# Output projections: a normed tile's transposes half a tile of products later, the last two tiles' inside the MLP's first unit, four normed-row buffers

## The chip, the cores and the metric

The kernel runs on one core of one Trainium2 chip. The metric is the device time of one execution in microseconds. Three timed runs of the kernel before gave 1408.19, 1409.34 and 1409.35 us, median 1409.34.

## What is computed (the reference, cut)

A two-layer encoder for one sequence of 512 positions with 1024 columns in float32. Layer 0 mixes tokens by dilated sliding-window attention, layer 1 by latent attention. Each mixer ends in an output projection that is added to the residual, and after it come a norm and a squared-ReLU MLP. The change lies at this seam, which occurs twice:

```python
def rms_norm(x, gain):
    xf = x.astype(jnp.float32)
    y = xf * lax.rsqrt(jnp.mean(xf * xf, axis=-1, keepdims=True) + EPS)
    return (y * gain.astype(jnp.float32)).astype(x.dtype)

def sq_relu_mlp(h, w1, w2):
    a = jax.nn.relu(h @ w1)
    return (a * a) @ w2

    for i in range(DEPTH):
        h = rms_norm(x, norm_mix[i])
        ...
            y = dilated_mixer(...)   # layer 0; ends in  o @ w_o
            y = mla_mixer(...)       # layer 1; ends in  o @ w_o
        x = x + y
        h = rms_norm(x, norm_ffn[i])
        x = x + sq_relu_mlp(h, ffn_w1[i], ffn_w2[i])
```

## The kernel before

**Numbers.** Every float32 operand of a product is split in two: `hi`, a rounded copy written by ACT, and `lo`, the rest, written by DVE as operand minus `hi`. Each product is made of three: hi·hi, hi·lo, lo·hi. Weights are loaded by SP as `raw` units of 256 rows by 512 columns (three buffers), split by `load_unit` (L158 on ACT, L159 on DVE) into `whi` and `wlo` (four buffers each).

**The projection (`project`, L920).** The 512 positions are four row tiles of 128. The output's 1024 columns are made in two blocks of 512. The second block holds all its weights, four units, and goes tile by tile: 8 slices of the inner dimension times 3 products, 24 products a tile (L183, from `block_groups`), into one of four `acc` banks. When a tile is done, DVE adds it to the residual (`resid`, L926), and `norm_tile` (L210) norms the row tile: ACT squares and sums (L138), DVE adds epsilon (L130), POOL raises to -1/2 (L133), DVE writes the normed row `xn` (L216). `norm_tile` returns a function `turn` that transposes the row: eight transposes on PE (L125) into two `tp` banks, of which there are only two, and out of each bank ACT copies `hi` (L226) and DVE subtracts `lo` (L227) into `hT_f`, the MLP's operand. The text calls the eight transposes of a row tile its turn.

**What sets the order.** A scheduler puts each engine's instructions in order by its own simulation. `tc.issue_after(ins)` binds the instructions issued inside it behind `ins` on the same engine. Before the change, tile 2's products were bound behind turn 0, tile 3's behind turn 1, and the MLP's first unit behind turn 2. Turn 3 was left to the scheduler.

**The MLP (`mlp`, L876).** Its first unit `up(0, 0)` takes its four weight units at once and works in two halves: first all products with columns 0 to 255 of `hT_f` (row tiles 0 and 1), 96 products of 256 columns, then those with columns 256 to 511 (row tiles 2 and 3). The later units follow one after another, with the second weight matrix loaded into `wqs` (on the memory of the projection's operand) and used by `down`.

Of the kernel before, what the change touches and what calls it, by code (L numbers as in the profile page):

```python
# [20 lines left out]
NT = S // P  # L21
# [67 lines left out]
def encoder_kernel(ctx: ExitStack, tc: tile.TileContext, x, norm_mix, norm_ffn, a_w_qkv, a_q_gain, a_k_gain,  # L89
# [3 lines left out]
    V, A, G, PE = nc.vector, nc.scalar, nc.gpsimd, nc.tensor  # L93
    uid = [0]
    marks = {}

    def nm(s):
        uid[0] += 1
        return f"{s}_{uid[0]}"
# [27 lines left out]
    def rstd_of(ss, n, add, name, out=None):  # L127

        v = st.tile([P, 8], F32, tag="rs_v", name=nm("rs_v"))
        V.tensor_scalar(v[:, :n], ss, add, None, op0=ALU.add)  # L130
        if out is None:
            out = st.tile([P, 8], F32, tag=name, name=nm(name))[:, :n]
        G.tensor_tensor(out, v[:, :n], nhalf[:, :n], op=ALU.pow)  # L133
        return out

    def mean_square(junk, x, dim, out):

        A.activation(junk, x, AF.Square, scale=1.0 / math.sqrt(dim), accum_out=out)  # L138
# [12 lines left out]
    def load_unit(src, nk, dims, n, home=None, raw=None):  # L151

        if raw is None:
            raw = load_raw(src, nk, dims, n)
        if home is None:
            home = [wp.tile([P, 2, 512], F32R, tag=t, name=nm(t)) for t in ("whi", "wlo")]
        hi, lo = home
        A.activation(hi[:, :nk, :n], raw[:, :nk, :n], AF.Copy)  # L158
        V.tensor_tensor(lo[:, :nk, :n], raw[:, :nk, :n], hi[:, :nk, :n].bitcast(F32), op=ALU.subtract)  # L159
        return hi, lo, nk  # L160

    def block_groups(units, groups, n, mm, outs=NT, halves=1, raws=None, order=None):

        accs = [acc_p.tile([P, 512], F32, tag="acc", name=nm("acc")) for _ in range(outs)]
        total = sum(u[1] for u in units)
        ui = 0
        kt0 = 0
        for gi, g in enumerate(groups):
            loaded = []
            for _ in range(g):  # L170
                src, nk, dims = units[ui]
                loaded.append(load_unit(src, nk, dims, n, raw=raws[ui] if raws else None))
                ui += 1
            first = [kt0 + sum(x[2] for x in loaded[:i]) for i in range(g)]
            kt0 = first[-1] + loaded[-1][2]
            steps = order or [(hv, o, u) for hv in range(halves) for o in range(outs) for u in range(g)]
            left = {o: g * halves for o in range(outs)}
            for hv, o, u in steps:
                hi, lo, nk = loaded[u]
                for j in range(nk):  # L180
                    kt = first[u] + j
                    for p_i, (lt, rt, oc) in enumerate(mm(o, kt, hi[:, j], lo[:, j], hv)):
                        PE.matmul(accs[o][:, oc], lhsT=lt, rhs=rt, start=(kt == 0 and p_i == 0 and hv == 0),  # L183
                                  stop=(kt == total - 1 and p_i == 2), skip_group_check=halves > 1)
                left[o] -= 1
                if gi == len(groups) - 1 and not left[o]:
                    yield o, accs[o]
            if gi < len(groups) - 1:
                yield None

    def run_block(units, groups, n, mm, evac, outs=NT, halves=1, order=None):
        for end in block_groups(units, groups, n, mm, outs, halves, order=order):
            if end is not None:
                evac(*end)

    def act_stationary(hT, n, own={}):

        def mm(r, kt, hi, lo, hv):
            a = own[kt] if kt in own else hT[:, kt]
            ah, al = (a[:, c, r * P:(r + 1) * P] for c in range(2))  # L200
            sl = slice(0, n)
            return [(ah, hi[:, :n], sl), (ah, lo[:, :n], sl), (al, hi[:, :n], sl)]
        return mm

    def w_units(w, n0, n):

        v = w.rearrange("(k p) c -> p k c", p=P)
        return [(v[:, k:k + 2, n0:n0 + n], 2, None) for k in range(0, v.shape[1], 2)]

    def norm_tile(r, src, gain_b, hT, pool, xn_bufs=2, xn_tag="xn"):  # L210

        ss = st.tile([P, 8], F32, tag="nss", name=nm("nss"))
        xn = pool.tile([P, D], F32, tag=xn_tag, name=nm("xn"), bufs=xn_bufs)
        mean_square(xn, src, D, ss[:, 0:1])
        rs = rstd_of(ss[:, 0:1], 1, EPS, "nrs")
        V.scalar_tensor_tensor(xn, src, rs, gain_b, op0=ALU.mult, op1=ALU.mult)  # L216

        def turn():
            for half in range(2):
                tp = tp_p.tile([P, 512], F32, tag="tp", name=nm("tp"))  # L220
                for j in range(4):
                    t = transpose(tp[:, j * P:(j + 1) * P], xn[:, (half * 4 + j) * P:(half * 4 + j + 1) * P])
                hi = hT[:, half * 4:half * 4 + 4, 0, r * P:(r + 1) * P]
                lo = hT[:, half * 4:half * 4 + 4, 1, r * P:(r + 1) * P]
                tv = tp.rearrange("p (k t) -> p k t", k=4)
                A.activation(hi, tv, AF.Copy)  # L226
                V.tensor_tensor(lo, tv, hi.bitcast(F32), op=ALU.subtract)  # L227
            return t.ins
        return turn
# [646 lines left out]
    def mlp(layer, w1, w2, hT_m, resid, pool, done):  # L876
        a2s = {}

        wqs = big.tile([P, 8, 2, 512], F32, tag="hT", name=nm("wqs"))

        def up(ch, grp):
            if grp == 0:
                if ch % 2:
                    a2s[ch] = pool.tile([P, 8, S], F32, tag="a2", name=nm("a2"))
                else:
                    a2s[ch] = x16.tile([P, 8, S], F32, tag="x16", name=nm("a2"))
            a2 = a2s[ch]
            c0 = ch * 1024 + grp * 512
            first = c0 == 0

            def mm(o, kt, hi, lo, hv, n=256 if first else 512):
                wh, wl = hi[:, o * P:(o + 1) * P], lo[:, o * P:(o + 1) * P]
                sl = slice(hv * n, hv * n + n)
                hh, hl = hT_m[:, kt, 0, sl], hT_m[:, kt, 1, sl]
                return [(wh, hh, sl), (wh, hl, sl), (wl, hh, sl)]

            def evac(o, acc):
                f = grp * 4 + o
                A.activation(a2[:, f], acc, AF.Relu)
                A.activation(a2[:, f], a2[:, f], AF.Square)  # L900

            run_block(w_units(w1, c0, 512), [4] if first else [1] * 4, 512, mm, evac, halves=2 if first else 1,
                      order=[(0, o, u) for u in range(4) for o in range(NT)] +
                      [(1, o, u) for o in range(NT) for u in range(4)] if first else None)

        def down(ch):
            a2 = a2s.pop(ch)
            wino(layer * 4 + ch, lambda i, j: a2[:, 4 * j:4 * j + 4, 256 * i:256 * i + 256],
                 w2[1024 * ch:1024 * ch + 1024, :], wqs, pool, resid, done if ch == 3 else None)

        with tc.issue_after(marks["turned"]):
            up(0, 0)
        up(0, 1)
        for ch in range(3):
            up(ch + 1, 0)
            down(ch)
            up(ch + 1, 1)
        down(3)

    def project(o_hl, w, resid, gain_src, hT_n, pool, g_name, begun=None):  # L920

        gain = gain_table(gain_src, D, g_name)

        def add(c, r, acc):
            sl = resid[:, r, 512 * c:512 * c + 512]
            V.tensor_tensor(sl, sl, acc, op=ALU.add)  # L926

        first = block_groups(w_units(w, 0, 512), [1, 1, 1, 1], 512, act_stationary(o_hl, 512)) if begun is None else begun
        for end in first:
            if end is not None:  # L930
                add(0, *end)
        second = block_groups(w_units(w, 512, 512), [4], 512, act_stationary(o_hl, 512))
        turns = []
        for r in range(NT):
            with ExitStack() as behind:
                if r > 1:
                    behind.enter_context(tc.issue_after(turns[r - 2]()))
                end = next(second)
            add(1, *end)
            turns.append(norm_tile(r, resid[:, r], gain, hT_n, pool))  # L940
        marks["turned"] = turns[NT - 2]()
        turns[NT - 1]()

    res_p = ctx.enter_context(tc.tile_pool(name="res_p", bufs=1, reuse_waits="tile"))
    resid = res_p.tile([P, NT, D], F32, name="resid")
# [300 lines left out]
```

## Time and profile before

| | |
|---|---|
| timed runs, median | 1409.34 us |
| profiled execution | 1411.71 us |
| its span, first to last instruction | 1409.9 us |
| mean granted clock | 0.999 |
| instructions | 18981 |

The prediction's durations come from the profiled execution, so its sum is made against 1411.71 us. Layer 0's projection ends at about 536 us of the span, layer 1's at about 1076 us. A row of the timeline gives start, length, engine, line, operation, output and inputs, count, and in brackets the engine's idle time before it and what ended it. Engines: PE multiplies and transposes, DVE and ACT work element by element, POOL does the powers, SP issues loads.

### The profile page before, as it was taken

The numbers are of one execution on the slowest core, as the hardware profiler recorded it, in microseconds if no ns is written. First come the engines' busy times: TensorE is split into PE (matmuls) and PEld (weight loads), VectorE is DVE, ScalarE is ACT, GpSimd is POOL, SyncE is SP. The second block draws the span as 40 slices with busy tenths as digits, with TensorE's granted clock in tenths as the row PEclk, the third lists the DMA queues.
The fourth block names the chain that finished last, engine by engine and source line by source line (L and its number), as shares of the span: only waits on it lengthen the run. The fifth ranks groups of instructions, "written<-read, shape, count | busy, mean of one in ns | idle before, by whom it ended". The sixth has DMA issues, their size and how long they took to land.

```text
span 1409.9 us, 18981 instructions
## 1 busy us (share of the span) xinstructions
PE 1374.4 (97%) x6852; PEld 1165.1 (83%) x6852; DVE 940.8 (67%) x1498; ACT 801.2 (57%) x1643; POOL 225.3 (16%) x240
## 2 busy tenths in 40 slices
PE   7999999999999999999999999899999999999998
PEld 6999878888889979888888878776768888888886
DVE  6885777787788744574655768788644465574747
ACT  6544778687786624553536455777523553644543
POOL 1110212121122001020200204523101020020201
PEclk9999999999999999999999999999999999999999
DMA  9535554655555538586683934200114758493835
GB/s 304 167 134 160 134 133 98 164 130 126 143 131 119 155 105 244 159 187 172 124 234 91 234 90 94 60 30 31 45 45 165 194 125 233 92 236 121 197 87 120
DMA packets 171774, 197.83 MB, mean 140 GB/s; under 512 B 59104, under 2 KB 109024, under 8 KB 171680
## 3 DMA queue, kind: packets, MB, share of 16 engines
q1 hardware_dynamic: 152496, 157.55, 37.8%
q0 software_dynamic: 19184, 39.07, 15.4%
q8 instruction: 54, 0.88, 0.3%
q14 instruction: 40, 0.33, 0.1%
HBM read 176.13 MB, written 7.86 MB: 130 GB/s over the span
## 4 chain that ended last, share of the span: by engine, by line
PE 80%; DVE 7%; DMA 5%; ACT 5%; issue 2%; SPq 0%; POOL 0%; ACTq 0%; DVEq 0%; POOLq 0%
PE acc L183 45%; PE sc L860 11%; PE tp L860 7%; DMA xT<-t 3%; PE tp L125 3%; PE sc L422 2%; PE acc L1157 1%; PE sc L1051 1%; PE acc L1133 1%; PE tp L422 1%; DVE wlo L803 1%; PE acc L422 1%; PE sco L702 1%; ACT junk L138 1%; PE sc L588 1%
## 5 line engine op out<-in xcount | busy, mean ns | idle before, releaser
L183 PE MATMUL acc<-whi,hT 128*128 128x512 f32 (+2 forms) x1208 | 378.0, 389 | 1.9 <-ACT hT L744 1.0
L183 PE MATMUL acc<-hT_f,whi 128*128 128x512 f32 (+1 forms) x1152 | 316.6, 366 | 0.0
L159 DVE TENSOR_TENSOR wlo<-raw,whi 128x1024 fp32r<-128x1024 f32 (+3 forms) x146 | 173.1, 1189 | 162.4 <-ACT whi L158 161.8
L183 PEld LDWEIGHTS acc<-whi,hT 128*128 128x128 f32 x1208 | 225.0, 189 | 43.5 <-ACT hT L744 1.8
L158 ACT ACTIVATE whi<-raw 128x1024 fp32r<-128x1024 f32 (+3 forms) x146 | 149.9, 1029 | 160.6 <-PE acc L183 64.4
L183 PEld LDWEIGHTS acc<-hT_f,whi 128*128 128x128 f32 x1152 | 207.5, 189 | 34.7
L183 PE MATMUL acc<-wlo,hT 128*128 128x512 f32 (+2 forms) x604 | 233.5, 387 | 0.7 <-DVE wlo L159 0.7
L803 DVE TENSOR_TENSOR wlo<-wqs,whi 128x1024 fp32r<-128x1024 f32 x112 | 137.7, 1232 | 112.4 <-ACT whi L802 112.2
L802 ACT ACTIVATE whi<-wqs 128x1024 fp32r<-128x1024 f32 x112 | 118.3, 1060 | 160.5 <-PE acc L183 66.2
L183 PE MATMUL acc<-hT_f,wlo 128*128 128x512 f32 (+1 forms) x576 | 204.1, 365 | 0.0
L860 PE MATMUL sc<-whi,asp 128*128 128x512 f32 x512 | 165.0, 389 | 1.2 <-DVE resid L834 1.2
L788 POOL DMA_DIRECT2D wqs<-in_ffn_w_dram x64 | 77.6, 1344 | 536.8 <-DVE wlo L803 356.5
L183 PEld LDWEIGHTS acc<-wlo,hT 128*128 128x128 f32 x604 | 113.8, 189 | 20.4 <-DVE wlo L159 1.1
L183 PEld LDWEIGHTS acc<-hT_f,wlo 128*128 128x128 f32 x576 | 108.2, 189 | 17.5
L860 PEld LDWEIGHTS sc<-whi,asp 128*128 128x128 f32 x512 | 96.1, 188 | 21.8 <-issue 2.0
L860 PE MATMUL tp<-whi,asp 128*128 128x512 f32 x352 | 112.1, 389 | 0.9 <-DVE resid L834 0.9
L133 POOL TENSOR_TENSOR qrs<-rs_v,nhalf 128x4 f32<-128x4 f32 x48 | 65.9, 1375 | 264.6 <-DVE rs_v L130 233.7
L860 PE MATMUL sc<-wlo,asp 128*128 128x512 f32 x256 | 99.6, 389 | 0.0
L296 ACT ACTIVATE qkT<-xT 128x1024 uint16<-128x1024 uint16 x48 | 56.5, 1183 | 43.0 <-DMA xT<-t 42.8
L860 PEld LDWEIGHTS tp<-whi,asp 128*128 128x128 f32 x352 | 66.1, 188 | 15.0 <-DVE resid L834 1.3
L860 PE MATMUL tp<-wlo,asp 128*128 128x512 f32 x176 | 68.1, 389 | 0.0
L138 ACT ACTIVATE junk<-acc 128x128 f32<-128x128 f32 x192 | 52.2, 272 | 11.0 <-PE acc L183 7.3
(236 smaller groups left out, 2189.0 us busy)
## 6 DMA issues: line engine op xcount, KB each, us to landing
wqs<-in_ffn_w_dram SPq DMA_DIRECT2D x80, 512.0 KB, 5.6
raw<-in_ffn_w_dram SPq DMA_DIRECT2D x64, 512.0 KB, 4.4
wqs<-in_ffn_w_dram POOLq DMA_DIRECT2D x64, 512.0 KB, 7.9
raw<-in_a_w_qkv_dram SPq DMA_DIRECT2D x96, 256.0 KB, 3.2
b<-in_a_w_qkv_dram SPq DMA_DIRECT2D x24, 384.0 KB, 5.7
vall<-vo POOLq DMA_DIRECT2D x24, 192.0 KB, 2.3
raw<-in_a_w_o_dram SPq DMA_DIRECT2D x8, 512.0 KB, 4.2
raw<-in_b_w_o_dram SPq DMA_DIRECT2D x8, 512.0 KB, 3.8
```

The source lines that it names most:

```text
L125: return PE.transpose(o, i, ident)
L133: G.tensor_tensor(out, v[:, :n], nhalf[:, :n], op=ALU.pow)
L138: A.activation(junk, x, AF.Square, scale=1.0 / math.sqrt(dim), accum_out=out)
L158: A.activation(hi[:, :nk, :n], raw[:, :nk, :n], AF.Copy)
L159: V.tensor_tensor(lo[:, :nk, :n], raw[:, :nk, :n], hi[:, :nk, :n].bitcast(F32), op=ALU.subtract)
L183: PE.matmul(accs[o][:, oc], lhsT=lt, rhs=rt, start=(kt == 0 and p_i == 0 and hv == 0), stop=(kt == total - 1 and p_i == 2), skip_group_che ...
L296: A.activation(dst, xT.rearrange("p (h c) t -> p c t h", h=2), AF.Copy)
L422: PE.matmul(banks[t][:, :VH], lhsT=lt, rhs=rt[:, j], start=(first and k == 0 and i_ == 0), stop=(k == 3 and i_ == 2), skip_group_check=True)
L788: marks["sum"] = nc.gpsimd.dma_start(t, src, accum_op=ALU.add).ins
L802: A.activation(hi, x, AF.Copy)
L803: V.tensor_tensor(lo, x, hi.bitcast(F32), op=ALU.subtract)
L860: PE.matmul(bk[t], lhsT=lt, rhs=rt[:, j], start=(first and k == 0 and i_ == 0), stop=(k == 3 and i_ == 2), skip_group_check=True)
```

## The change

It gives `block_groups` a table `between`: after the step with a given number the function in it is called (a turn), bound behind the step's last product, and the next step's products are bound behind the turn's last transpose. A step is one row tile (or one group of output columns, in the MLP) with one weight unit, 6 products. In the projection's second block, turn 0 now stands after step 9, which is half of tile 2, and turn 1 after step 13, half of tile 3. Turns 2 and 3 are handed to the MLP and stand after steps 3 and 11 of its first unit. The bonds of before are taken out. `xn` gets four buffers instead of two.

```diff
-    def block_groups(units, groups, n, mm, outs=NT, halves=1, raws=None, order=None):
+    def block_groups(units, groups, n, mm, outs=NT, halves=1, raws=None, order=None, between={}):
...
-            for hv, o, u in steps:
+            cut = None
+            for i, (hv, o, u) in enumerate(steps):
                 hi, lo, nk = loaded[u]
-                for j in range(nk):
...
+                with ExitStack() as behind:
+                    if cut is not None:
+                        behind.enter_context(tc.issue_after(cut))
+                        cut = None
+                    for j in range(nk):
+                        kt = first[u] + j
+                        for p_i, (lt, rt, oc) in enumerate(mm(o, kt, hi[:, j], lo[:, j], hv)):
+                            last = PE.matmul(accs[o][:, oc], lhsT=lt, rhs=rt, start=(kt == 0 and p_i == 0 and hv == 0),
+                                             stop=(kt == total - 1 and p_i == 2), skip_group_check=halves > 1)
+                if i in between:
+                    with tc.issue_after(last.ins):
+                        cut = between[i]()
...
             run_block(w_units(w1, c0, 512), [4] if first else [1] * 4, 512, mm, evac, halves=2 if first else 1,
                       order=[(0, o, u) for u in range(4) for o in range(NT)] +
-                      [(1, o, u) for o in range(NT) for u in range(4)] if first else None)
+                      [(1, o, u) for o in range(NT) for u in range(4)] if first else None,
+                      between={3: marks["turns"][2], 11: marks["turns"][3]} if first else {})
...
-        with tc.issue_after(marks["turned"]):
-            up(0, 0)
+        up(0, 0)
...
-        second = block_groups(w_units(w, 512, 512), [4], 512, act_stationary(o_hl, 512))
         turns = []
-        for r in range(NT):
-            with ExitStack() as behind:
-                if r > 1:
-                    behind.enter_context(tc.issue_after(turns[r - 2]()))
-                end = next(second)
-            add(1, *end)
-            turns.append(norm_tile(r, resid[:, r], gain, hT_n, pool))
-        marks["turned"] = turns[NT - 2]()
-        turns[NT - 1]()
+        second = block_groups(w_units(w, 512, 512), [4], 512, act_stationary(o_hl, 512),
+                              between={9: lambda: turns[0](), 13: lambda: turns[1]()})
+        for r, acc in second:
+            add(1, r, acc)
+            turns.append(norm_tile(r, resid[:, r], gain, hT_n, pool, xn_bufs=4))
+        marks["turns"] = turns
```

The scheduler makes its own order of this. Three places of layer 0 show it; layer 1 has the same pattern. In the rows, `acc_5060`, `acc_5061` and `acc_5062` are the banks of row tiles 1, 2 and 3; `whi_5065`, `whi_5071`, `whi_5077` and `whi_5083` the four weight units of the projection; `xn_5113`, `xn_5146`, `xn_5193` and `xn_5240` the normed rows of tiles 0 to 3.

**First place: PE, between tile 1 and tile 2.** Before, turn 0 (`xn_5113`) stands between tile 1's last product and tile 2's first:

```order
L183 MATMUL acc_5060<-whi_5083,hT_4802 128x512 x2
L183 MATMUL acc_5060<-wlo_5084,hT_4802 128x512
L183 MATMUL acc_5060<-whi_5083,hT_4802 128x512
L125 MATMUL tp_5153<-ck,xn_5113 128x128 x4
L125 MATMUL tp_5160<-ck,xn_5113 128x128 x4
L183 MATMUL acc_5061<-whi_5065,hT_4802 128x512
L183 MATMUL acc_5061<-wlo_5066,hT_4802 128x512
```

Now, with the end of the first half of tile 3 ahead of it:

```order
L188 MATMUL acc_5062<-whi_5071,hT_4802 128x512
L188 MATMUL acc_5062<-wlo_5072,hT_4802 128x512
L188 MATMUL acc_5062<-whi_5071,hT_4802 128x512 x2
L188 MATMUL acc_5062<-wlo_5072,hT_4802 128x512
L188 MATMUL acc_5062<-whi_5071,hT_4802 128x512
L125 MATMUL tp_5165<-ck,xn_5113 128x128 x4
L125 MATMUL tp_5172<-ck,xn_5113 128x128 x4
L188 MATMUL acc_5061<-whi_5077,hT_4802 128x512
L188 MATMUL acc_5061<-wlo_5078,hT_4802 128x512
```

Turn 0 moved behind 24 products: the first half of tile 2 and, as the scheduler pulled it forward, the first half of tile 3. The second half of tile 2, turn 1 and the second half of tile 3 follow.

**Second place: ACT, from tile 1's square to the evacuation of the turns.** Before (`whi_5287`, `whi_5293`, `whi_5299`, `whi_5305` are the four weight units of the MLP's first unit):

```order
L138 ACTIVATE xn_5146,nss_5145<-resid 128x1024
L226 ACTIVATE hT_f_5019<-tp_5153 128x4x128
L226 ACTIVATE hT_f_5019<-tp_5160 128x4x128
L226 ACTIVATE hT_f_5019<-tp_5200 128x4x128
L138 ACTIVATE xn_5193,nss_5192<-resid 128x1024
L226 ACTIVATE hT_f_5019<-tp_5207 128x4x128
L158 ACTIVATE whi_5287<-raw_5285 128x1024
L158 ACTIVATE whi_5293<-raw_5291 128x1024
L158 ACTIVATE whi_5299<-raw_5297 128x1024
```

Now (`whi_5259`, `whi_5265`, `whi_5271`, `whi_5277` are the same four units):

```order
L138 ACTIVATE xn_5146,nss_5145<-resid 128x1024
L158 ACTIVATE whi_5259<-raw_5257 128x1024
L158 ACTIVATE whi_5265<-raw_5263 128x1024
L234 ACTIVATE hT_f_5019<-tp_5165 128x4x128
L234 ACTIVATE hT_f_5019<-tp_5172 128x4x128
L234 ACTIVATE hT_f_5019<-tp_5212 128x4x128
L138 ACTIVATE xn_5193,nss_5192<-resid 128x1024
L234 ACTIVATE hT_f_5019<-tp_5219 128x4x128
L158 ACTIVATE whi_5271<-raw_5269 128x1024
L158 ACTIVATE whi_5277<-raw_5275 128x1024
L138 ACTIVATE xn_5240,nss_5239<-resid 128x1024
L234 ACTIVATE hT_f_5019<-tp_5305 128x4x128
```

Two weight splits of the MLP stand ahead of turn 0's evacuation now. DVE has the two subtractions that go with them at the same place, behind the writing of tile 1's row.

**Third place: PE, where turn 2 (`xn_5193`) and the MLP's first unit meet.** Before, the unit (`acc_5281` and `acc_5282` are two of its banks) starts behind the turn:

```order
L183 MATMUL acc_5062<-wlo_5084,hT_4802 128x512
L183 MATMUL acc_5062<-whi_5083,hT_4802 128x512
L125 MATMUL tp_5247<-ck,xn_5193 128x128 x4
L125 MATMUL tp_5254<-ck,xn_5193 128x128 x4
L183 MATMUL acc_5281<-hT_f_5019,whi_5287 128x256 x2
L183 MATMUL acc_5282<-hT_f_5019,whi_5287 128x256 x2
```

Now the turn stands inside the unit, behind its first 40 products (`acc_5253` and `acc_5256` are its banks):

```order
L188 MATMUL acc_5256<-hT_f_5019,whi_5259 128x256 x2
L188 MATMUL acc_5256<-hT_f_5019,wlo_5260 128x256
L125 MATMUL tp_5305<-ck,xn_5193 128x128 x4
L125 MATMUL tp_5312<-ck,xn_5193 128x128 x4
L188 MATMUL acc_5253<-hT_f_5019,whi_5265 128x256 x2
L188 MATMUL acc_5253<-hT_f_5019,wlo_5266 128x256
```

Turn 3 follows 32 products later, its two banks parted by two products. On SP one raw load of the MLP's second unit moved ahead of the eight `wqs` loads.

More of the change, by code (lines that the diff above doesn't have):

```diff
@@ L177, in block_groups @@
             left = {o: g * halves for o in range(outs)}
-            for hv, o, u in steps:
+            cut = None
+            for i, (hv, o, u) in enumerate(steps):
                 hi, lo, nk = loaded[u]
-                for j in range(nk):
[L181 to L184, printed above, removed]
+                with ExitStack() as behind:
[10 more added lines that the diff above has]
+                        cut = between[i]()
                 left[o] -= 1
@@ L189, in block_groups, with run_block @@
                 yield None
-    def run_block(units, groups, n, mm, evac, outs=NT, halves=1, order=None):
-        for end in block_groups(units, groups, n, mm, outs, halves, order=order):
+    def run_block(units, groups, n, mm, evac, outs=NT, halves=1, order=None, between={}):
+        for end in block_groups(units, groups, n, mm, outs, halves, order=order, between=between):
             if end is not None:
```

## The prediction

> **What bounds the kernel now.** I read the page first, then PE's waits, then the chain of waits and PE's timeline around them.
>
> ```profile
> PE 1374.4 (97%) x6852; PEld 1165.1 (83%) x6852; DVE 940.8 (67%) x1498; ACT 801.2 (57%) x1643; POOL 225.3 (16%) x240
> PE 80%; DVE 7%; DMA 5%; ACT 5%; issue 2%; SPq 0%; POOL 0%; ACTq 0%; DVEq 0%; POOLq 0%
> ```
>
> PE is busy for 97% of the span and carries 80% of the chain that ended last. So this change can gain only where PE stands still or runs slowly, or lose where it makes PE stand still; it removes no product. The answer on PE's waits (who waits for what: total us, times, longest) puts one wait of the code that is touched near the top:
>
> ```profile
> PE tp L125 <- DVE xn L362: 9.5, 1, 9.5
> PE tp L125 <- DVE xn L216: 3.0, 2, 2.1
> ```
>
> The 9.5 us are the kernel's start. The second row is the one at issue: the transposes of L125 wait twice, 3.0 us together, for the normed row that DVE writes on L216. Each wait belongs to one of the two output projections. PE's timeline has them (start, length, engine, line, operation, count, and in brackets PE's idle time before and what ended it):
>
> ```profile
> 521.30 0.39 PE L183 MATMUL acc<-whi,hT 128*128 128x512 f32 x1
> 522.62 1.09 PE L125 MATMUL tp<-ck,xn 128*128 128x128 f32 x8 [0.94 <-DVE xn L216]
> ...
> 1058.56 0.39 PE L183 MATMUL acc<-whi,hT 128*128 128x512 f32 x1
> 1061.02 1.07 PE L125 MATMUL tp<-ck,xn 128*128 128x128 f32 x8 [2.07 <-DVE xn L216]
> ```
>
> The chain of waits through the same two places (start, length, piece):
>
> ```profile
> 521.28 1.30 DVE xn L216
> 522.58 0.04 issue
> 522.62 1.09 PE tp L125 x8
> 523.72 5.49 PE acc L183 x24
> 529.21 0.88 PE tp L125 x8
> 530.09 5.45 PE acc L183 x24
> 535.54 0.87 PE tp L125 x8
> 536.41 8.99 PE acc L183 x75
> ...
> 546.28 57.57 PE acc L183 x309
> ...
> 1059.60 1.29 DVE xn L216
> 1060.89 0.14 issue
> 1061.02 1.07 PE tp L125 x8
> 1062.09 7.06 PE acc L183 x24
> 1069.15 0.87 PE tp L125 x8
> 1070.02 5.46 PE acc L183 x24
> ```
>
> Two things are to be seen. A row tile is 24 products in 5.45 us, so 0.227 us each, and after the first turn (a tile's eight transposes, 0.87 us) PE never waits again: the turns of tiles 1 to 3 find their rows ready. And the tile at 1062.09 took 7.06 us for the same 24 products that take 5.46 us at 1070.02. The stretches of one us there show why (the last three columns are granted clock, DMA share, GB/s):
>
> ```profile
> 1061.00:1062.00 1.00, 0.98 (x9) 1.00 (x10) 0.33 (x2) 0.31 (x1) 0.56 (x1) 1.00 0.00 0
> 1062.00:1063.00 1.00, 1.00 (x4) 0.78 (x4) 1.00 (x2) 0.77 (x2) 0.00 (x0) 0.54 0.08 16
> 1063.00:1064.00 1.00, 1.00 (x4) 0.74 (x3) 1.00 (x3) 0.00 (x0) 0.00 (x0) 0.50 0.00 0
> 1064.00:1065.00 1.00, 1.00 (x4) 0.81 (x3) 0.21 (x1) 0.00 (x0) 0.00 (x0) 0.50 0.00 0
> 1065.00:1066.00 1.00, 1.00 (x4) 0.80 (x4) 0.00 (x0) 0.00 (x0) 0.00 (x0) 0.75 0.00 0
> 1066.00:1067.00 1.00, 1.00 (x6) 0.80 (x5) 0.00 (x0) 0.00 (x0) 0.00 (x0) 1.00 0.00 0
> ```
>
> After the wait of 2.07 us the granted clock was about half for some 3.4 us. After the wait of 0.94 us nothing of the kind is seen: its 24 products took 5.49 us. So the second wait costs twice, as idle time and as slow products behind it.
>
> **The first wait (layer 0).** The last product of tile 1 starts at 521.30; the next instruction could start 0.23 us later, at 521.53. The turn starts at 522.62. Lost: 1.09 us. After the change this turn stands behind the first half of tile 2 and, by the order of the changed kernel, the first half of tile 3 too: 24 products, so at 521.53 + 5.45 = 526.98. Its row is ready at 522.58, 4.4 us earlier. The wait goes, whole.
>
> **The second wait (layer 1).** By the same reckoning PE is free at 1058.79, the turn starts at 1061.02: 2.23 us lost. After the change the turn is due at 1058.79 + 5.45 = 1064.24; the row is ready at 1060.89. That wait goes as well, with 3.35 us to spare.
>
> **The slow stretch behind it.** 7.06 - 5.46 = 1.60 us. If the standstill brought it on, it goes too; between nothing and all of 1.60 us I take all, since in this trace it follows the longest wait after the start and no shorter one. The nearest shorter wait is one of 1.6 us for L691, and the clock in the stretch behind it is whole:
>
> ```profile
> PE sco L702 <- ACT pT L691: 1.6, 1, 1.6
> ...
> 271.00:274.00 3.00, 3.00 (x19) 2.62 (x19) 1.76 (x5) 1.29 (x2) 0.00 (x0) 1.00 0.64 195
> ```
>
> The Trainium skill, "TensorE: Matmul & The Clock Gate", section "Why this matters for your kernels", sets the bar higher: it is one idle window, gaps of more than some 3 us, that drops PE to half clock. The trace differs: here a gap of 2.07 us stood before it. By the rule as written the slow stretch would have another cause and might stay; that is the first rival below.
>
> **What is late next: the turn of tile 1.** It needs the two tp banks, which turn 0 filled, and so turn 0's evacuation (two copies on ACT, L226; two subtractions on DVE, L227). On both engines the new order puts two weight splits of the MLP's first unit (L158, L159) ahead of that evacuation. The durations:
>
> ```profile
> 531.70 2.22 ACT L158 ACTIVATE whi<-raw 128x1024 fp32r<-128x1024 f32 x2
> 534.26 1.07 ACT L158 ACTIVATE whi<-raw 128x1024 fp32r<-128x1024 f32 x1 [0.34 <-PE acc L183]
> 536.01 1.09 ACT L226 ACTIVATE hT_f<-tp 128x512 fp32r<-128x512 f32 x2 [0.69 <-PE tp L125]
> ...
> 533.64 3.49 DVE L159 TENSOR_TENSOR wlo<-raw,whi 128x1024 fp32r<-128x1024 f32 x3
> 537.64 1.28 DVE L227 TENSOR_TENSOR hT_f<-tp,hT_f 128x512 fp32r<-128x512 f32 x2
> ```
>
> In layer 0's clock: a weight buffer of the projection is free when tile 3 is done with its group, for the first at 521.53 + 18 x 0.227 = 525.6, for the second at 527.0; I add an estimated 0.25 us for a product's end to be seen (it lasts 0.39 us by its row, 0.16 more than its step). ACT splits at 525.9 and 527.25, ends 528.3, and copies turn 0 by 529.4. DVE (1.16 us a split) ends the second one at 529.5 and turn 0's subtractions at 530.15 and 530.8. PE has meanwhile done turn 0 (to 527.85) and the second half of tile 2 (12 products, 2.72 us), so it wants the first bank at 530.57 and the second at 531.0. Margins of 0.4 and 0.2 us: no wait, but no comfort either. Bounds: 0 to, if every split ran one split (1.1 us) late, 0.9 us in each layer. I take 0.
>
> **What is late after that.** The MLP's first unit starts at 531.44 + 2.72 = 534.16 and reads only tiles 0 and 1 in its first half. Turn 1's first bank is copied by 531.75 and subtracted by 532.45, the second by 534.2; that one holds the inner slices of the third weight group on, due behind 30 products of 0.12 us (8.99 us for 75), at 537.8. The third and fourth split end at 534.5 and 535.6 on ACT (due at 537.8 and 543.7), their subtractions at 537.3 and 538.5 (due at 541.5 and later). Turn 2 is due at 539.0, its row done at 535.4; turn 3 at 543.7, its row (square on ACT from 536.2, behind the fourth split) at 540.6; the unit's second half needs both at 547.4, turn 3 being evacuated by about 546. Each is covered by over 1 us.
>
> **DMAs and queues.** The change issues no DMA more. The fourth raw buffer of the unit is loaded when the first split is subtracted: ready by 528.2 now, 534.8 before, where ACT waited for it:
>
> ```profile
> 512.80 22.47 SPq L148 DMA_DIRECT2D raw<-in_ffn_w_dram  x2
> ...
> 538.69 1.06 ACT L158 ACTIVATE whi<-raw 128x1024 fp32r<-128x1024 f32 x1 [1.59 <-DMA raw<-in_ffn_w_dram]
> ```
>
> SP issues one raw load ahead of the wqs loads instead of between them; wqs is read first after the 57.57 us of products that start at 546.28, so some 50 us cover it. POOL's work is the same four powers in each layer, ahead of its accumulating loads. The two more xn buffers let tile 2's row be written before turn 0 is read; without them the later turn would hold up the square on ACT. Their cost is memory; a first write waits at most for loads of earlier stages, long landed. I count nothing.
>
> **Small change.** The turns cost what they cost, except that turn 3 is split in two by two products. A switch back from transposes costs 0.32 - 0.23 = 0.09 us (first product to second):
>
> ```profile
> 529.84 0.48 PE L183 MATMUL acc<-whi,hT 128*128 128x512 f32 x1
> 530.16 0.39 PE L183 MATMUL acc<-wlo,hT 128*128 128x512 f32 x1
> ```
>
> Between 0 and a whole turn of 0.87 us I take 0.09, twice.
>
> **Sum.** 1.09 + 2.23 + 1.60 - 0.18 = 4.74 us gained. Behind both places PE runs on without a wait (57.57 us at 546.28), so the gain is carried to the end. The profiled execution took 1411.71 us, its span 1409.9, so it would be 1406.97. The timed runs' median is 1409.34, 2.37 lower; I take the same gain off it: **1404.6 us**.
>
> **Rivals.**
> 1. The slow stretch is not in the timed runs, or is not due to the wait. For it: two timed runs at 1409.3 and one at 1408.19, 1.15 us less, as if one lacked most of it; one profile can't say how often it comes. Against: it stands right behind the wait. Gain 3.32 - 0.18 = 3.14: 1406.2 us.
> 2. Turn 1 waits for its banks. For it: margins of 0.2 to 0.4 us worked out from durations. Against: weights that landed long before. 0.9 us in both layers: gain 2.94, 1406.4 us.
> 3. The wait only moves: PE stands as long at turn 0 or turn 1 as before, since ACT and DVE have the same work to do there. Against: rows ready 3.35 and 4.4 us ahead. 1409.3 us.
> 4. Slower. Turn 1 waits so long for the banks behind the splits that it brings the half clock upon both layers: 2 x (2.1 idle + 1.6 slow) = 7.4 us lost against 4.9 gained, 1411.8 us. It decides from evacuations some 2.3 us later than reckoned; ACT and DVE would have to be late by two whole splits.
>
> **Chances.** Forecast 0.52; rival 1 0.25; rival 2 0.12; rival 3 0.07; rival 4 0.04. A measurement of this kernel can tell about 0.2%, 2.8 us, from no change, that is a time under 1406.5. The forecast lies clear of it (0.50 of 0.52), rival 1 just beyond it (0.15 of 0.25), rival 2 on it (half). So faster 0.71, same 0.25, slower 0.04. The range runs from the forecast less 1 us of scatter (the timed runs spread by 1.16) to past rivals 1 and 2: 1403.6 to 1408.0; beyond it lie rivals 3 and 4 and the tails, under 0.2.
>
> **What the changed profile would show.** The row of PE's waits for xn of L216 (3.0 us, twice) gone or under 0.2 us. The two tiles behind turn 0 at 0.227 us a product in both layers, granted clock 1.00. The MLP's first product 2.0 us earlier after tile 1 in layer 0 (one turn moved, 1.1 gained). No wait of tp for DVE's or ACT's hT. I am wrong if tp waits for hT at turn 1, if a clock of 0.5 shows up elsewhere, or if the wait goes and the time stays.

## The result, and the profile after

| | before | changed |
|---|---|---|
| timed runs, median (11 each, in turn on one chip) | 1409.35 us (1408.19 to 1411.98) | 1405.97 us (1404.90 to 1408.83) |
| ratio, 95% interval | | 0.9977 (0.9969 to 0.9985) |
| profiled execution | 1411.71 us | 1405.79 us |
| its span | 1409.9 us | 1404.0 us |

The changed kernel is faster by 3.4 us of medians, 0.24%, and the interval lies clear of 1. Two single runs far out of line, one of the kernel before beside the experiments (1976.57 us) and one of the kernel with only the first turns later (3571.52 us), are left out of every median below. The first lines of its PE waits (who waits for what: total us, times, longest):

```profile
PE tp L125 <- DVE xn L370: 9.7, 1, 9.7
PE sc L1055 <- DVE ks L1109: 2.4, 2, 1.2
```

The row of 3.0 us in two waits for the normed row is gone, and no wait for the evacuation (`hT_f`) has come in its place. The chain of waits through layer 0 (start, length, piece):

```profile
509.48 16.62 PE acc L188 x72
526.10 0.87 PE tp L125 x8
526.98 2.77 PE acc L188 x12
529.75 0.87 PE tp L125 x8
530.62 7.53 PE acc L188 x52
538.15 0.87 PE tp L125 x8
539.02 3.83 PE acc L188 x32
542.85 0.44 PE tp L125 x4
543.28 0.24 PE acc L188 x2
543.52 0.44 PE tp L125 x4
```

There is nothing but PE in it, with turn 3 in two pieces as the order has it. Layer 1 reads alike:

```profile
1045.59 16.62 PE acc L188 x72
1062.21 0.87 PE tp L125 x8
1063.09 2.74 PE acc L188 x12
...
1079.63 0.44 PE tp L125 x4
```

Its stretches of 5 us (length, then busy time and instructions of PE, weight loads, DVE, ACT and POOL, then granted clock, DMA share, GB/s) show PE busy throughout, at full clock:

```profile
1060.00:1065.00 5.00, 5.00 (x28) 4.23 (x27) 3.66 (x4) 3.09 (x4) 0.00 (x0) 1.00 0.15 27
1065.00:1070.00 5.00, 5.00 (x30) 4.32 (x29) 3.89 (x7) 3.52 (x6) 0.55 (x1) 1.00 0.57 184
```

**Where the time of the two profiles went.** I compare the moments at which the same work is done. Three more pieces of the chain of the kernel before are needed, the starts of both projections' second blocks and the end of the turns in layer 1:

```profile
510.51 8.02 PE acc L183 x34
...
1047.78 11.19 PE acc L183 x48
...
1086.23 5.87 PE acc L183 x49
```

The changed kernel enters layer 0's block at 509.48 instead of 510.51: 1.03 us ahead before the change has done anything. In the old kernel four turns and 75 products of the MLP are done at 546.28. In the new one 74 are done with turn 3 at 543.96, and one more (0.12 us) makes 544.08. It is 2.20 us ahead there, so **layer 0 brought 1.17 us** (forecast 1.09 - 0.09 = 1.00). It enters layer 1's block 2.19 us ahead, so nothing was lost between, and stands at 1080.07 + 0.12 = 1080.19 against 1086.23: 6.04 ahead, so **layer 1 brought 3.85 us** (forecast 2.23 + 1.60 - 0.09 = 3.74). Together that is 5.02 against the forecast 4.74, in two profiles. The medians show only 3.4. The two pieces of turn 3 take 0.44 us each, together no more than a turn in one piece (0.87). So the question for the runs is which part of the 5.02 the usual execution doesn't have.

### The profile page after: what moved, and what is told of

It reads as the page before. It is cut to its first block, busy times and chain, and to the rows that moved or that the text cites. A ratio compares the mean times of both kernels' runs of the same rounds, so it can differ in the third digit from the quotient of the medians.

```text
span 1404.0 us, 18978 instructions
## 1 busy us (share of the span) xinstructions
PE 1371.9 (98%) x6852; PEld 1164.1 (83%) x6852; DVE 940.9 (67%) x1498; ACT 801.2 (57%) x1643; POOL 225.3 (16%) x240
## 4 chain that ended last, share of the span: by engine, by line
PE 81%; DVE 7%; ACT 4%; DMA 4%; issue 2%; SPq 0%; POOL 0%; ACTq 0%; DVEq 0%
PE acc L188 46%; PE sc L868 11%; PE tp L868 7%; PE tp L125 3%; DMA xT<-t 2%; PE sc L430 2%; PE acc L1161 1%; PE sc L1055 1%; DVE wlo L811 1%; PE acc L1137 1%; PE tp L430 1%; PE sco L710 1%; PE acc L430 1%; PE sco L706 1%; ACT junk L138 1%
```

## The experiments

Each kernel was timed in five rounds beside the kernel before; kernels of one group below ran on the same chip with common runs of it. "Mean clock" is the mean granted clock of a run, given to three places; the half clock of 3.4 us is worth some 0.001 of it.

### Does every execution have the slow stretch?

**The kernel before, unchanged, again** (no edit).

> The kernel before once more, to see how often the half-clock stretch behind layer 1's wait comes. Theory (it comes in a part of the executions only, which is why the median gained 3.4 us and not 4.7): time 1409.4 +- 0.5; the mean clock of some runs is 0.999 or less and of others 1.0, and the runs with the whole clock are about 1.6 us shorter; wait of PE for xn again 0.9 and 2.1 us. Rival (the stretch comes in every execution, and the changed kernel loses about 1.4 us elsewhere): all runs of this kernel show 0.999 or less and lie within 1 us of each other.

Measured: 1409.03 us, ratio 0.9995 (0.9987 to 1.0004). The profile has the stretch again. The chain after turn 0 in layer 1 (7.02 us for 24 products), and the stretch of 5 us there, at a clock of 0.75:

```profile
1059.33 7.02 PE acc L183 x24
```

```profile
1060.00:1065.00 5.00, 5.00 (x18) 4.04 (x17) 1.41 (x3) 0.00 (x0) 0.00 (x0) 0.75 0.00 0
```

Of the 11 runs six have a mean clock of 0.999 and a median of 1409.82, five have 1.000 and 1408.88. All runs of the kernel before beside the experiments, with these 11, are 110: 48 lie below 1.000, median 1410.08; 62 at 1.000, median 1408.70. The times of the two groups overlap, but their medians are 1.4 us apart, near the 1.60 of the slow stretch. **Many executions do not have the stretch.**

**The changed kernel, again** (no edit), and **with two `xn` buffers**:

```diff
-            turns.append(norm_tile(r, resid[:, r], gain, hT_n, pool, xn_bufs=4))
+            turns.append(norm_tile(r, resid[:, r], gain, hT_n, pool))
```

> The whole change once more, beside the same with two buffers. Theory: 0.9977 of the kernel before, 3.3 us less; clock 1.0 in most runs. Rival (two buffers are better): 0.5 us or more above the two-buffer kernel of the same call.

> The whole change with two buffers, on one chip with the whole change. Theory: the same within 0.4 us, since no instruction waits for a buffer in either. Rival: 0.5 us or more below it, as the two earlier results from different calls would have it (1405.08 against 1405.97).

Measured: 1405.54 us, ratio 0.9976 (0.9967 to 0.9985), and 1405.55, 0.9977 (0.9968 to 0.9986). The two-buffer kernel had also been run earlier, in 5 runs:

> The whole change with two xn buffers as before. Theory: tile 2's square comes at about 530.7 of the span, after turn 0 (done 527.9), and tile 3's after turn 1, so the buffers are never waited for: 1406.0 us, as the whole change. Rival (my prediction's sentence that without the two more buffers the later turn holds up the square on ACT): ACT's square waits for PE's transposes, and the time lies 0.5 to 2 us above the whole change.

Measured: 1405.08 us, 0.9967 (0.9955 to 0.9979), no wait for `xn` or `hT_f`. The buffers make no difference. With the first timing of the changed kernel these are 38 runs, all without the standstill: 28 at mean clock 1.000, median 1405.55; 10 below, median 1405.70. Here a lower mean clock costs nothing. The profile of the changed kernel shows one place where it can come from, the idle last 2 us, where PE has no work:

```profile
1402.00:1404.00 2.00, 0.00 (x0) 0.00 (x0) 0.00 (x0) 0.00 (x0) 0.00 (x0) 0.62 0.03 9
```

So a run's mean clock alone doesn't tell the stretch; its mean clock with its time says more. If the idle end lowers the mean clock as often in the kernel before, 10 runs of 38, the 62 of 110 at 1.000 leave the stretch in about a quarter of the executions: 1 - (62/110)/(28/38) = 0.24, an estimate from these counts.

**At mean clock 1.000 the two kernels are 1408.70 - 1405.55 = 3.15 us apart**, about the two waits without the stretch, 1.09 + 2.23 - 0.18 = 3.14. That it fits to 0.01 is luck: on the one chip of these repetitions, which ran both kernels, it is 1408.32 - 1405.55 = 2.77, with 16 runs of each.

### Is the stretch due to the standstill?

**Layer 1's wait filled** with nine products into a bank that nobody reads (this adds work that isn't in the reference), and **filled in part** with three; bound between tile 1's last product and turn 0:

```diff
...
+                if r == 2 and begun is None:
+                    with tc.issue_after(marks["last"]):
+                        idle = sc_p.tile([P, 512], F32, tag="sc", name=nm("idle"))
+                        for k in range(9):    # in the second kernel 3
+                            m = PE.matmul(idle, lhsT=o_hl[:, 0, 0, 0:P], rhs=o_hl[:, 0, 0], start=True, stop=True)
+                    with tc.issue_after(m.ins):
+                        t = turns[r - 2]()
...
```

> The kernel before, with nine products of 512 columns that nobody reads put into layer 1's wait ahead of turn 0: the row comes no earlier, but PE is busy (9 x 0.227 = 2.0 us of the 2.23). Theory (the standstill brings the half clock, in about half of the executions): no slow stretch behind turn 0, the tile of 24 products in about 5.5 us, nearly all runs with clock 1.0, median 1408.9 to 1409.1, about 0.6 us under the kernel before. Rival (the stretch has another cause): half of the runs at 0.999 as before, median 1409.6.

> The same with three products: the standstill in layer 1 is cut from 2.1 to about 1.4 us at an unchanged turn. Theory (what counts is the length of the standstill; one of 1.6 us elsewhere in this kernel never brought it): stretch rare or gone, 1.0 in nearly all runs, median about 1409.0. Rival (any standstill there does it): half of the runs at 0.999, 1409.6.

**The wait lengthened**: layer 1's row of tile 0 is written twice.

```diff
...
+        if again:
+            V.scalar_tensor_tensor(xn, src, rs, gain_b, op0=ALU.mult, op1=ALU.mult)
...
```

> The kernel before with tile 0's row in layer 1 written twice by DVE, so that turn 0 waits about 1.4 us longer, 3.5 us in all. Theory (a longer standstill makes the half clock sure): all runs at 0.999, 1409.0 + 1.4 + 1.5 = 1411.9 us. Rival (the half clock comes by chance, whatever the length): half of the runs at 0.999, median 1409.6 + 1.4 = 1411.0.

The three chains of layer 1. Filled (turn 0 never waits):

```profile
1058.02 2.04 PE idle L941 x9
1060.06 0.03 issue
1060.09 1.07 PE tp L125 x8
1061.15 5.49 PE acc L183 x24
```

Filled in part (a standstill of 1.4 us is left):

```profile
1059.60 1.07 PE tp L125 x8
1060.67 5.49 PE acc L183 x24
```

Lengthened (3.4 us), where not only tile 2 but the turn itself runs slowly, 1.94 us instead of 1.07:

```profile
1059.16 1.94 PE tp L125 x8
1061.10 6.12 PE acc L183 x24
```

and its clock, which falls before the turn starts at 1059.16:

```profile
1055.00:1060.00 5.00, 1.56 (x8) 1.13 (x7) 3.92 (x6) 1.29 (x4) 2.09 (x2) 0.89 0.00 0
1060.00:1065.00 5.00, 5.00 (x21) 4.21 (x20) 2.14 (x3) 1.19 (x2) 0.00 (x0) 0.77 0.02 3
```

| longest standstill at layer 1's turn 0 | median, us | ratio (95%) | runs below clock 1.000 |
|---|---|---|---|
| filled | 1409.05 | 1.0000 (0.9991 to 1.0009) | 4 of 11 |
| 1.4 us | 1408.76 | 0.9999 (0.9990 to 1.0007) | 3 of 11 |
| 2.1 us (kernel before, all) | 1409.24 | | 48 of 110 |
| 3.4 us | 1410.87 | 1.0018 (1.0009 to 1.0027) | 10 of 11 |

Whether the filled kernels gain the stretch in time can't be read from their medians: what is sought is a few tenths. Their profiles run tile 2 at full speed, but two profiles prove little, since one with the whole wait (below, layer 0 alone) does so too. Nearly all their runs were expected at 1.000; the 4 and 3 of 11 below it can't be told from 48 of 110 or from the 10 of 38 without this standstill. The lengthened kernel decides by its clock: 10 of 11. Its time doesn't decide: the interval, 1.0009 to 1.0027 of 1409.13, runs from 1410.4 to 1412.9 and holds both the rival's 1411.0 and the theory's 1411.9. In its profile the slow work costs 0.87 us at the turn and 0.63 at tile 2, together the 1.5 that the theory took. So **the standstill brings the half clock on**, not always at 2.1 us, nearly always at 3.4.

### Which part of the change brings what?

**Turns 0 and 1 later, turns 2 and 3 as before**, against the changed kernel:

```diff
-                      between={3: marks["turns"][2], 11: marks["turns"][3]} if first else {})
+                      between={})
...
-        up(0, 0)
+        with tc.issue_after(marks["turned"]):
+            up(0, 0)
...
-        marks["turns"] = turns
+        marks["turned"] = turns[NT - 2]()
+        turns[NT - 1]()
```

> Turns 0 and 1 half a tile later with four buffers, turns 2 and 3 as before (turn 2 ahead of the MLP's first unit). Theory: PE's waits at turn 0 go in both layers, but turn 2 is now due at 534.2 of the span while its row is done at about 535.4: a new wait for xn of L224 of about 1.2 us in each layer, so 2.4 of the 3.4 us are given back: 1408.3 us. Rival (the first two turns are all that counts, the move into the MLP is worth nothing): 1406.0, as the whole change.

Measured: 1407.98 us, ratio 0.9991 (0.9982 to 0.9999). A new wait takes the place of the old, in both layers, at turn 2 ahead of the MLP:

```profile
PE tp L125 <- DVE xn L224: 2.1, 2, 1.1
```

Tile 2's row is not ready where turn 2 stood; the first two turns can move only if the third moves too. Two of the 11 runs, 1410.33 and 1410.78, lie over 2 us above the median, at a mean clock of 0.998. The one profile, a run at 1.000, doesn't show what slowed them.

**Turns 2 and 3 into the MLP, turns 0 and 1 as before**, also against the changed kernel:

```diff
-        second = block_groups(w_units(w, 512, 512), [4], 512, act_stationary(o_hl, 512),
-                              between={9: lambda: turns[0](), 13: lambda: turns[1]()})
-        for r, acc in second:
-            add(1, r, acc)
+        second = block_groups(w_units(w, 512, 512), [4], 512, act_stationary(o_hl, 512))
+        for r in range(NT):
+            with ExitStack() as behind:
+                if r > 1:
+                    behind.enter_context(tc.issue_after(turns[r - 2]()))
+                end = next(second)
+            add(1, *end)
```

> Turns 2 and 3 inside the MLP's first unit, turns 0 and 1 as before, four buffers. Theory: both waits at turn 0 stay (0.9 and 2.1 us) and turns 2 and 3 were already covered: 1409.4 us, no change within 0.5 us. Rival (the turns inside the unit save time themselves, by a border with fewer switches): 1 to 2 us less than before.

Measured: 1409.74 us, ratio 1.0003 (0.9994 to 1.0012). The old wait stays, and so does the slow stretch:

```profile
PE tp L125 <- DVE xn L224: 3.0, 2, 2.1
```

```profile
1059.08 1.06 PE tp L125 x8
1060.14 7.10 PE acc L188 x24
```

**The whole change in one layer, the other as before**, against the changed kernel:

```diff
+        late = begun is not None     # second kernel: begun is None
+        marks["late"] = late
...
-                              between={9: lambda: turns[0](), 13: lambda: turns[1]()})
+                              between={9: lambda: turns[0](), 13: lambda: turns[1]()} if late else {})
```

and the bonds of before for the layer that isn't `late`.

> The whole change in layer 0 only, layer 1 as before. If the waits are worth what the sum says: 1.09 - 0.09 = 1.0 us under the kernel before, 1408.3 us if that stands at 1409.3; the wait for xn stays once (2.1 us, layer 1), and the half clock behind it still comes in some of the executions, so that the gain at equal clock and the gain of the medians are the same 1.0. If the later turns gained by something other than the wait (the loads or splits moved with them): half of the whole change's gain, 1.6 us.

> The whole change in layer 1 only, layer 0 as before. If the waits are worth what the sum says: 2.23 - 0.09 = 2.1 us at full clock, and some 0.3 to 0.7 us more of the medians because the half clock goes with it: 2.4 to 2.8 us under the kernel before, 1406.5 to 1406.9 us if that stands at 1409.3; the wait for xn stays once (0.9 us, layer 0), and no half clock in the profile. If the half clock had another cause than this wait: 2.1 us and clocks below 1.0 as often as before. If the later turns gained by something other than the wait: half of the whole change's gain, 1.6 us.

Measured: layer 0 alone 1408.32 us, ratio 0.9992 (0.9983 to 1.0000), 0.6 us of medians; layer 1 alone 1406.69, 0.9981 (0.9973 to 0.9990), 2.2 us. The intervals hold 0 to 2.4 and 1.4 to 3.8 us; the expected 1.0 and 2.4 to 2.8 lie in them, but so does 1.6 for each, and the two medians add up to 2.8 of 3.4. The runs scatter by more than is sought: with layer 1 alone five lie from 1404.15 to 1405.44 and seven from 1406.63 to 1407.87, with runs at mean clock 1.000 in both. Part of the scatter comes from work ahead of the change: the four profiles of the changed kernel, with four or two buffers, enter layer 0's block at 508.37, 509.26, 509.48 and 510.06 us and took 1404.84, 1405.58, 1405.79 and 1405.80. What parted those twelve runs is not shown. What each kernel keeps is clearer in its waits. Layer 0 alone:

```profile
PE tp L125 <- DVE xn L224: 2.1, 1, 2.1
```

Layer 1 alone:

```profile
PE tp L125 <- DVE xn L224: 0.9, 1, 0.9
```

The kernel with layer 0 alone also gives the counterpart to the kernel before: the same wait of 2.1 us, and this time no slow stretch behind it. Its chain in layer 1:

```profile
1045.95 11.19 PE acc L188 x48
...
1059.19 1.06 PE tp L125 x8
1060.26 5.48 PE acc L188 x24
...
1082.81 2.27 PE acc L188 x19
```

This answers the question that the two profiles left. From the start of the block to the end of the turns layer 1 takes 1082.81 - 1045.95 = 36.86 us here, against 1080.19 - 1045.59 = 34.60 in the changed kernel. So without the stretch the change brings 2.26 us in layer 1, and with the 1.17 of layer 0 3.43 in all; the other 1.59 of the 5.02 were the stretch. Nor is it 1.6 in each layer.

### How thin is the margin at turn 1's banks?

**Turn 0 and turn 1 back to back**, behind the first half of tile 3, with no other product of the block allowed between:

```diff
-                        cut = None
+                        cut = cut if len(between) == 1 else None
...
-                              between={9: lambda: turns[0](), 13: lambda: turns[1]()})
+                              between={13: lambda: (turns[0](), turns[1]())[1]})
```

> The changed kernel, but turn 0 and turn 1 back to back behind the first half of tile 3, without the 12 products between them. If turn 1 needs turn 0's banks as the prediction reckons: turn 0 ends at about 529.7 us in layer 0, its banks are free at about 531.1 and 532.1, so PE waits for tp by 1.4 us and once more by 0.5 us in each layer, about 4 us over the changed kernel: 1409.5 us, about the time before; a wait of tp for hT in PE's waits; little or no half clock, as no standstill reaches 2 us. If the two banks are evacuated while PE still fills them and the 12 products between the turns aren't needed: no wait, 1405.5 us.

Measured: 1415.81 us (5 runs), ratio 1.0046 (1.0034 to 1.0058), 6.9 us over the kernel before and 10.3 over the changed one (1405.54 in its repetition); mean clock 0.997 in every run. Its PE waits and timeline:

```profile
PE tp L125 <- DVE hT_f L235: 6.7, 2, 3.4
```

```profile
527.84 1.04 PE L125 MATMUL tp<-ck,xn 128*128 128x128 f32 x8
532.24 1.96 PE L125 MATMUL tp<-ck,xn 128*128 128x128 f32 x8 [3.37 <-DVE hT_f L235]
...
537.55 0.64 PE L188 MATMUL acc<-hT_f,whi 128*128 128x256 f32 x4
...
1073.44 1.25 PE L125 MATMUL tp<-ck,xn 128*128 128x128 f32 x8 [3.38 <-DVE hT_f L235]
...
1078.87 0.64 PE L188 MATMUL acc<-hT_f,whi 128*128 128x256 f32 x4
```

The wait is 3.4 us and not the 1.4 expected. DVE's timeline shows the reason: tile 2 is now finished before turn 0, so its row and both splits stand ahead of turn 0's subtractions:

```profile
528.03 1.28 DVE L224 SCALAR_TENSOR_TENSOR xn<-resid,nrs,g_ffn 128x1024 f32<-128x1024 f32 x1 [0.66 <-POOL nrs L133]
529.23 2.35 DVE L159 TENSOR_TENSOR wlo<-raw,whi 128x1024 fp32r<-128x1024 f32 x2
531.50 1.28 DVE L235 TENSOR_TENSOR hT_f<-tp,hT_f 128x512 fp32r<-128x512 f32 x2
```

And the half clock follows in both layers (5 us with the granted clock):

```profile
530.00:535.00 5.00, 2.76 (x11) 2.57 (x12) 3.60 (x6) 1.27 (x3) 0.00 (x0) 0.73 0.63 193
...
1075.00:1080.00 5.00, 5.00 (x21) 4.14 (x20) 2.88 (x4) 2.27 (x3) 0.00 (x0) 0.66 0.25 89
```

From turn 1 to the MLP's first product there are one turn and 12 products; in the changed kernel that takes 533.19 - 529.59 = 3.60 us:

```profile
529.59 1.03 PE L125 MATMUL tp<-ck,xn 128*128 128x128 f32 x8
...
533.19 0.64 PE L188 MATMUL acc<-hT_f,whi 128*128 128x256 f32 x4
```

Here it takes 5.31 and 5.43, so 1.71 and 1.83 us are lost to slow products and the second bank. 3.37 + 3.38 + 1.71 + 1.83 = 10.3 us, as much as the whole difference to the changed kernel. This is the fourth rival's mechanism, at a place where it does decide.

## Why the prediction was right, and where its size was off

- **The first wait, 1.09 us, and the second, 2.23.** Right: the row of both waits is gone. Without the slow stretch the profiles give 1.17 + 2.26 = 3.43 us for the two, and the runs at mean clock 1.000 about 3, where the sum has 3.14.
- **The slow stretch, 1.60 us.** This is the term that was mis-sized. The prediction took "all, since in this trace it follows the longest wait after the start and no shorter one". The cause is right (it comes nearly always with the longer standstills, and the profiles of the filled kernels have none), and so is its length where it comes. But it comes only in a part of the executions: in three of the four profiles with the 2.1 us wait, and by the estimate from the mean clocks in about a quarter. The median of the runs before, 1409.24, lies nearer to the runs at mean clock 1.000 (1408.70) than to the others (1410.08): over all runs the kernels are 1409.24 - 1405.57 = 3.67 us apart against 3.15 at 1.000, so it is worth some 0.5 us of the medians. How often it comes isn't settled, since the mean clock is also lowered at the kernel's idle end and four profiles are few. The prediction had the hint in hand: it read the run at 1408.19 as one that "lacked most of it", as its first rival, and still priced the forecast by the profiled execution, which was 2.4 us over the median. The result, 1405.97, lies next to that rival's 1406.2 and is 1.4 us above the forecast; the gain of 3.4 is inside the range because the range was drawn past that rival.
- **The skill's rule.** The Trainium skill, "TensorE: Matmul & The Clock Gate", section "Why this matters for your kernels", asks for a gap of more than some 3 us. Here 2.07 us was enough at times and 3.4 us nearly always. The same page, section "What's actually happening", has a window of some 3.4 us that runs free of the kernel, so that the same kernel meets it at another phase each time. That agrees with one standstill that has a slow stretch behind it in some executions and none in others; what the window counts as idle, no run here shows.
- **Turn 1's banks.** Right, with the margins as thin as said. The evacuation in the changed profile, layer 0 (a row of a timeline counts from the start of its first instruction, so it can overlap the row before, and turn 1 stands at 529.59 there and at 529.75 in the chain):

```profile
527.10 1.07 ACT L234 ACTIVATE hT_f<-tp 128x512 fp32r<-128x512 f32 x2
```

```profile
528.37 1.28 DVE L235 TENSOR_TENSOR hT_f<-tp,hT_f 128x512 fp32r<-128x512 f32 x2
```

The second bank is free at 529.65 and the first some 0.6 us before; turn 1 starts at 529.59 and needs the second half a turn later, at 530.0. The margins are about 0.5 and 0.4 us (0.4 and 0.2 were worked out). Without the 12 products between the turns and with tile 2's row ahead, the same dependence costs 10.3 us.
- **The other rivals.** No wait of `tp` for `hT_f`, no slow stretch elsewhere, no wait that merely moved. It moves only if turn 2 stays ahead of the MLP (1.1 us in each layer).
- **Turn 3 in two pieces, 0.18 us, and queues and DMAs at nothing.** The loss of 0.18 didn't come: the pieces took 0.44 us each, and the two waits, 3.32 together, brought 3.43. What brings the other 0.11 isn't shown. That leaves little room for a cost of queues and DMAs.
- **The buffers.** Wrong in a side remark: "without them the later turn would hold up the square on ACT". With two buffers neither waits nor time change.
- **The 2.37 us between the profile and the median.** Taking the same gain off both was the same error: a part of that distance was the stretch itself, and 1.03 us of the difference between the profiles lay ahead of the change.

## What to carry to other kernels

A transpose that waits for a row's norm should stand where the row is long done, and the whole sequence behind it has to move along: moving the first turns alone only moved the wait to the third. Before a loss seen in one profile is priced in full, the times of single runs should be looked at together with their mean clock: a loss that comes in part of the executions is worth less in the median. A move that closes up two users of the same banks needs the evacuation's place in the other engines' order worked out first; half a tile of other products between them is what kept it free here.

## What the runs showed of the hardware

A standstill of PE of 2.07 us and the eight transposes behind it were followed by some 3.4 us at half clock, in three profiles of four. Standstills of up to 1.6 us were followed by it in no profile, those of 3.4 us (three, in two kernels) each time. The half clock may begin within the standstill, where it costs nothing: in the lengthened kernel the granted clock of 1055 to 1060 us is 0.89 already, and the slow work cost 1.50 us against 1.60 behind the shorter wait. The granted clock also fell to 0.62 in the idle last 2 us of one execution, which lowers a run's mean clock and not its speed. And a granted clock of 1.00 is no proof of full speed. In the kernel before, behind the standstill of 9.52 us at the start, the first eight transposes take 1.97 us, and three products of 384 columns step 0.95 us at 14.59 but 0.53 from 18.10, while the granted clock is given as 1.00 from 10 to 20 us. Why the two differ there is open.
